# A decoder trunk on one core: the first product reads x times g, its norm is applied at the end, and set-up steps move

## The chip, the cores and the metric

The kernel runs on one core of a Trainium2 chip. The metric is the device time of one execution in microseconds (us). A core has a matrix engine (PE in the profile, with its weight loads under PEld), a vector engine (DVE), a scalar engine (ACT), a general one (POOL) and a sequencer that issues most transfers (SP). Each runs its own instructions strictly in the order in which the program wrote them, and waits on semaphores for the others.

## The reference, cut to what matters

```python
def rmsnorm(x, g):                       # x: (1, 256, 1024)
    y = x * lax.rsqrt(jnp.mean(x * x, axis=-1, keepdims=True) + EPS)
    return y * g

for l in range(2):
    h = rmsnorm(x, norm_mix_g[l])
    proj = h @ w_in[l]                   # (1024 x 6664): conv q/k, v, gates, attention q, k, v ...
    x = x + mixer(proj) @ w_out[l]       # mLSTM and sliding window attention side by side
    x = x + sqrelu_mlp(rmsnorm(x, norm_mlp_g[l]), w_up[l], w_down[l])
return rmsnorm(x, final_norm_g)
```

The columns of `w_in` that give the values `mv` are multiplied first. Row t of a product h @ w is r[t] * ((x * g) @ w)[t], where r is the reciprocal root of the row's mean square, so that r can be applied to the product instead of to x.

## The kernel before, in words

256 tokens stand in two tiles of 128 rows (`tt` 0 and 1), the 1024 features in eight blocks of 128 (`kt`). Weights come in pieces of 128 rows by 1024 columns (512 KB). A piece passes through three steps: SP loads it into a raw buffer (four of these, `N_RAW`); ACT rounds it to fp32r, the high part (`hi`, line 152); DVE subtracts that from the raw piece, the low part (`lo`, line 127, or by halves in line 134). When the low part is done the raw buffer is free, and the transfer of the piece four places on is issued (`pump_dma`). There are seven pairs of high and low buffers (`N_SPL`). Activations are split in the same way (`xh`, `xl`). A product is three matmuls: high by high, high by low, low by high. In `xs` (lines 220 to 222) the activations are stationary and 512 columns stream; in `ws` (lines 234 to 236) the weights are stationary and 256 tokens stream.

The work is a list of slots written out by hand; one slot is what one piece serves. `run_slots` (line 191) writes them out one after the other for all engines: first what was put `at` a slot, then casts of pieces up to `target` (four pieces beyond what the slot needs, or `limits`), then `late` steps, then subtractions, then `at_last`, then the slot's matmuls, then what was put `after` it. The order in this list is the order in each engine's queue.

The start, which the change touches:

- `setup_start` (line 400) issues on SP: x of tile 0 in two halves, the row of g, the first pieces, x of tile 1, and then in `small_loads` (line 388) eleven small loads. PE runs 26 and 16 small matmuls without use to warm up.
- `first_norm` (line 524) squares tile 0, takes the reciprocal root on POOL (line 349), scales x by it (line 532), transposes on PE (line 537) and splits into `xh` (ACT, line 541, with g as the scale) and `xl` (DVE, line 547). Tile 1 follows while the first slots run.
- The first product, `mv`, has slots 0 to 7. In the first half its order is by token tile (`head="t"`): slots 0 and 1 take pieces 0 to 3 for tile 0, slots 2 and 3 the same for tile 1. Slots 4 to 7 take one piece each. Its four banks are read out by `mv_evac` after slot 7: ACT takes two (line 603), DVE two (line 601).
- Slots 8 to 11 are the product `kv` (four pieces, `kk` and `kv` banks, which are the same banks that `mv_evac` empties). Slots 12 to 19 are `aq`.
- `setup_small` (line 426, at slot 2) and `setup_cols` (line 439, at slot 4) prepare masks, columns of the convolution and a table of biases, which POOL writes out and SP reads back from slot 12 on (line 462).

Of the kernel before, what the change touches and what calls it, by code (L numbers as in the profile page):

```python
# [17 lines left out]
P = 128  # L18
T = 256
# [23 lines left out]
def trunk(ctx: ExitStack, tc: tile.TileContext, x, norm_mix_g, w_in, conv_w, conv_b, b_igate, b_fgate,  # L43
# [41 lines left out]
    n_dma, n_split = [0], [0]  # L85

    def piece(w, kt, c0):
        def load(raw):
            nc.sync.dma_start(raw[:, :1024], w[kt * P : (kt + 1) * P, c0 : c0 + 1024])
# [33 lines left out]
    def pump_lo():  # L123
        for j in los:
            raw, n = raws.pop(j), pieces[j][1]
            hi, lo = pc[j]
            nc.vector.tensor_tensor(lo[:, :n], raw[:, :n], hi[:, :n].bitcast(F32), op=ALU.subtract)  # L127
# [198 lines left out]
    def hc(hf):  # L326
        return slice(hf * 512, (hf + 1) * 512)
# [55 lines left out]
    vm = const.tile([P, 2, 4, 257], F32, name="vm")  # L383
    S0 = {}

    N_WARM = (26, 16, 8)

    def small_loads():
        S0["b8"] = big8()
        rows = S0["rows"] = S0["b8"][:80, 0, 0:P]  # L390
        rb = S0["rb"] = const.tile([NB_BUCKETS, 16], F32, name="rb")
        nc.sync.dma_start(rb, rel_bias)
        for l in range(DEPTH):
            nc.sync.dma_start(gb_bias[:, l, 0:4], b_igate[l].partition_broadcast(P))
            nc.sync.dma_start(gb_bias[:, l, 4:8], b_fgate[l].partition_broadcast(P))
            nc.sync.dma_start(sink[:, l, :], attn_sinks[l].partition_broadcast(P))
            nc.sync.dma_start(rows[40 * l : 40 * l + 32, :], conv_w[l].rearrange("j (m c) -> (j m) c", c=P))
            nc.sync.dma_start(rows[40 * l + 32 : 40 * l + 40, :], conv_b[l].rearrange("(m c) -> m c", c=P))

    def setup_start():  # L400
        grow = big8()[:8, 0, 0:P]
        nc.sync.dma_start(X[:, 0, 0:512], xv[:, 0, 0:512])
        nc.sync.dma_start(X[:, 0, 512:], xv[:, 0, 512:])
        nc.sync.dma_start(grow, norm_mix_g[0].rearrange("(k c) -> k c", c=P))
        for i in range(N_RAW):
            if i == 3:
                nc.sync.dma_start(X[:, 1, :], xv[:, 1, :])
            pump_dma()
# [6 lines left out]
        nc.vector.memset(mask, 0.0)  # L415
        pw = psA()
        for _ in range(N_WARM[0]):
            nc.tensor.matmul(pw[:, :P], mask, mask, start=True, stop=True)
        pg = psA()
        nc.tensor.transpose(pg[:, :8], grow, ident[:8, :8])  # L420
        S0["gcol"] = const.tile([P, KT], F32, name="gcol")
        S0["pg"], S0["pw"] = pg, pw
        for _ in range(N_WARM[1]):
            nc.tensor.matmul(pw[:, :P], mask, mask, start=True, stop=True)

    def setup_small():
        nc.vector.tensor_copy(identb, ident)
        nc.gpsimd.affine_select(
            out=mask, in_=mask, pattern=[[1, P]], compare_op=ALU.is_ge, fill=NEG, base=0, channel_multiplier=-1)
        nc.gpsimd.memset(vm[:, :, :, 256:257], 1.0)  # L430
        z = tmp()
        nc.gpsimd.memset(z, 0.0)
        nc.scalar.copy(Rs, z[:, 0:384])
        for r in (0, 32):
            nc.gpsimd.affine_select(out=z[r : r + 32, 0:4], in_=z[r : r + 32, 0:4], pattern=[[-1, 4]],
                                    compare_op=ALU.not_equal, fill=1.0, base=0, channel_multiplier=1)
        nc.scalar.copy(sel, z[:, 0:4])

    def setup_cols():
        pt = psB()  # L440
        nc.tensor.transpose(pt[:, :80], S0["rows"], ident[:80, :80])
        nc.vector.tensor_copy(cw, pt[:, :80])
# [3 lines left out]
        nc.vector.tensor_copy(rbT, pt[:16, :NB_BUCKETS])
        Et = S0["b8"][:16, 1, 0:384]
        nc.gpsimd.memset(Et, NEG)
        bk = t5_bucket(np.arange(P))
        nc.gpsimd.tensor_copy(Et[:, 127 : 127 + 16], rbT[:, 0:16])  # L450
        for b in range(16, NB_BUCKETS):
            idx = np.nonzero(bk == b)[0]
            if len(idx):
                lo, n = int(idx[0]), len(idx)
                nc.gpsimd.tensor_copy(Et[:, 127 + lo : 127 + lo + n], rbT[:, b : b + 1].to_broadcast([16, n]))
        ed = dram.tile([16, 384], F32, name="ed")
        nc.gpsimd.dma_start(ed, Et)
        S0["ed"], S0["tz"] = ed, [big8((P, 8, T)) for _ in range(2)]
# [64 lines left out]

    def first_norm(st, xtag, nxt):

        xh, xl = st["hT"] = xT_tiles(xtag)
        N = [Norm(0), Norm(1)]
        gcol, xn, pts = S0["gcol"], {}, {}

        def scale(tt, hf):  # L530
            xn[tt, hf] = tmp()
            nc.vector.tensor_scalar(xn[tt, hf], X[:, tt, hc(hf)], N[tt].r[:, :1], None, op0=ALU.mult)

        def tr(tt, hf):
            pts[tt, hf] = psB()
            for j in range(4):
                nc.tensor.transpose(pts[tt, hf][:, j * P : (j + 1) * P], xn[tt, hf][:, j * P : (j + 1) * P], ident)

        def hi(tt, ks):
            for k in ks:  # L540
                nc.scalar.activation(xh[:, k, tt * P : (tt + 1) * P], pts[tt, k // 4][:, k % 4 * P : (k % 4 + 1) * P],  # L541
                                     AF.Copy, scale=gcol[:, k : k + 1])

        def lo(tt, ks):
            for k in ks:
                s = slice(tt * P, (tt + 1) * P)
                nc.vector.scalar_tensor_tensor(xl[:, k, s], pts[tt, k // 4][:, k % 4 * P : (k % 4 + 1) * P],
                                               gcol[:, k : k + 1], xh[:, k, s].bitcast(F32), op0=ALU.mult,
                                               op1=ALU.subtract)

        N[0].square(0)
        N[0].square(1, "dve")
        N[0].rstd()
        nc.scalar.copy(gcol, S0["pg"][:, :8])
        pump_hi(0, 0)
        scale(0, 0)
        tr(0, 0)
        for _ in range(N_WARM[2]):
            nc.tensor.matmul(S0["pw"][:, :P], mask, mask, start=True, stop=True)
# [8 lines left out]
        lo(0, (2, 3))
        pump_hi(0, 2)
        N[1].square(0)  # L570
        N[1].square(1)
        pump_lo()
        N[1].rstd()
        scale(0, 1)
        pump_hi(0, 3)
        scale(1, 0)
        pump_lo()
        scale(1, 1)

        def tr_all(tt, hf):  # L580
            tr(tt, hf)
            hi(tt, range(4 * hf, 4 * hf + 4))
            lo(tt, range(4 * hf, 4 * hf + 4))

        for i in range(4):
            limits[nxt + i] = 3 + max(0, i - 1)
        slots[nxt + 1][0].insert(2, call(lambda: tr_all(1, 0)))
        slots[nxt + 2][0].insert(1, call(lambda: tr_all(0, 1)))
        slots[nxt + 2][0].insert(4, call(lambda: tr_all(1, 1)))


    def mixer(l, ta, tb):
        w = w_in[l]
        st = {}
        s_mv = xs_group(st, "mv", "hT", w, MV0, head="t")

        def mv_evac(tt, hf):
            o = vm[:, tt, 2 * hf : 2 * hf + 2, 0:256]
            i = st[("mv", tt, hf)].rearrange("p (h c) -> p h c", h=2)
            if hf:  # L600
                nc.vector.tensor_copy(o, i)
            else:
                nc.scalar.copy(o, i)
# [462 lines left out]
    for l in range(DEPTH):  # L1066
# [95 lines left out]
```

## Time and profile before

| what | value |
|---|---|
| median of three runs | 883.37 us (883.11 to 884.58) |
| the profiled execution's own time | 884.32 us |
| its span on the core | 882.5 us |
| DVE busy, ACT busy | 572.4 us, 468.2 us |
| POOL busy | 128.3 us |
| read from memory | 153.23 MB |

The profile is of one execution. A row of a timeline gives the start, the duration, the engine, the line, what is written from what, how many in a row, and in brackets how long the engine was idle before and who ended that. A view of waits sums such idle times. A view by windows gives each engine's busy time in stretches that the reader names, with the clock that TensorE was granted (PEclk) and the share of the transfer engines. The 1.8 us between span and own time lie outside the program.

### The profile page before, as it was taken

What the parts mean: (1) busy time and instruction counts of PE and PEld (TensorE: products, weight loads), DVE (VectorE), ACT (ScalarE), POOL (GpSimd) and SP (SyncE); (2) the same over time, 40 slices, a digit from 0 to 9 for tenths busy, and PEclk for the clock granted to TensorE, in tenths of its full rate; (3) what the DMA queues carried; (4) which work ended last, traced back from release to release, by engine and by line L of the source; (5) the groups of instructions that cost most, each with busy time, mean ns of one, the idle gap of its engine ahead of it and who ended that gap; (6) DMA issues with size and microseconds to landing.
All of it is one profiled execution on the core that took longest, in us unless ns stands there. A gap on an engine that the chain in (4) does not pass through costs nothing.

```text
span 882.5 us, 15073 instructions
## 1 busy us (share of the span) xinstructions
PE 868.5 (98%) x5929; PEld 789.6 (89%) x5929; DVE 572.4 (65%) x928; ACT 468.2 (53%) x771; POOL 128.3 (15%) x164
## 2 busy tenths in 40 slices
PE   7999999999999999999999999999999999999996
PEld 5899889999989999998889997999998899999985
DVE  5758879666666654546574788876667764737363
ACT  5657776654355554544355557764634453636352
POOL 1360534120000000000002435322000000000000
PEclk9999999999999999999999999999999999999999
DMA  6875435445556747474655455354564466555621
GB/s 217 288 246 186 144 120 167 141 147 158 177 191 202 248 133 240 133 242 136 219 171 189 149 186 163 109 160 144 148 223 157 146 225 225 194 188 188 194 96 48
DMA packets 50711, 155.28 MB, mean 176 GB/s; under 512 B 7912, under 2 KB 10192, under 8 KB 50640
## 3 DMA queue, kind: packets, MB, share of 16 engines
q1 hardware_dynamic: 49456, 150.69, 52.8%
q0 software_dynamic: 896, 3.17, 1.0%
q8 instruction: 46, 0.75, 0.4%
q10 hardware_dynamic: 288, 0.46, 0.1%
q14 instruction: 25, 0.20, 0.1%
HBM read 153.23 MB, written 1.07 MB: 175 GB/s over the span
## 4 chain that ended last, share of the span: by engine, by line
PE 92%; DVE 3%; issue 2%; ACT 1%; POOL 1%; DMA 0%; POOLq 0%; SPq 0%; DVEq 0%; ACTq 0%
PE pa L220 13%; PE pa L221 13%; PE pa L222 12%; PE pa L235 10%; PE pa L234 10%; PE pa L236 10%; PE pb L235 5%; PE pb L234 5%; PE pb L236 5%; PE pb L859 1%; PE pb L322 1%; PE pb L879 1%; DVE lo L127 1%; PE pb L919 1%; PE pb L832 1%
## 5 line engine op out<-in xcount | busy, mean ns | idle before, releaser
L127 DVE TENSOR_TENSOR lo<-raw,hi 128x1024 fp32r<-128x1024 f32 (+1 forms) x276 | 332.0, 1226 | 137.5 <-ACT hi L152 134.4
L152 ACT CAST hi<-raw 128x1024 fp32r<-128x1024 f32 (+1 forms) x280 | 286.1, 1049 | 184.0 <-PE pa L222 48.1
L234 PE MATMUL pa<-xh,hi 128*128 128x256 f32 x864 | 246.4, 285 | 0.0
L235 PE MATMUL pa<-xl,hi 128*128 128x256 f32 x864 | 242.6, 281 | 0.0
L236 PE MATMUL pa<-xh,lo 128*128 128x256 f32 x864 | 241.7, 280 | 0.0
L234 PEld LDWEIGHTS pa<-xh,hi 128*128 128x128 f32 x864 | 162.7, 188 | 0.9 <-issue 0.3
L235 PEld LDWEIGHTS pa<-xl,hi 128*128 128x128 f32 x864 | 162.9, 189 | 0.3
L236 PEld LDWEIGHTS pa<-xh,lo 128*128 128x128 f32 x864 | 162.8, 188 | 0.0
L220 PE MATMUL pa<-hi,xh 128*128 128x512 f32 (+1 forms) x384 | 149.9, 390 | 1.8 <-ACT xh L541 1.8
L221 PE MATMUL pa<-lo,xh 128*128 128x512 f32 (+1 forms) x384 | 148.1, 386 | 0.5 <-DVE lo L127 0.4
L222 PE MATMUL pa<-hi,xl 128*128 128x512 f32 (+1 forms) x384 | 147.8, 385 | 0.0
L234 PE MATMUL pb<-xh,hi 128*128 128x256 f32 x384 | 107.6, 280 | 0.0
L235 PE MATMUL pb<-xl,hi 128*128 128x256 f32 x384 | 107.6, 280 | 0.0
L236 PE MATMUL pb<-xh,lo 128*128 128x256 f32 x384 | 107.3, 280 | 0.0
L220 PEld LDWEIGHTS pa<-hi,xh 128*128 128x128 f32 x384 | 72.2, 188 | 15.4 <-ACT xh L541 2.0
L222 PEld LDWEIGHTS pa<-hi,xl 128*128 128x128 f32 x384 | 72.1, 188 | 15.4
L221 PEld LDWEIGHTS pa<-lo,xh 128*128 128x128 f32 x384 | 72.2, 188 | 15.2 <-DVE lo L127 1.6
L349 POOL TENSOR_TENSOR sm<-sm,mhalf 128x1 f32<-128x1 f32 x9 | 6.6, 731 | 500.0 <-DVE sm L348 500.0
L235 PEld LDWEIGHTS pb<-xl,hi 128*128 128x128 f32 x384 | 72.3, 188 | 1.8
L234 PEld LDWEIGHTS pb<-xh,hi 128*128 128x128 f32 x384 | 72.2, 188 | 1.7
L236 PEld LDWEIGHTS pb<-xh,lo 128*128 128x128 f32 x384 | 72.3, 188 | 0.0
L220 PE MATMUL pa<-hi,b 128*128 128x512 f32 x124 | 48.8, 394 | 0.0
(210 smaller groups left out, 986.1 us busy)
## 6 DMA issues: line engine op xcount, KB each, us to landing
raw<-in_w_in SPq DMA_DIRECT2D x104, 512.0 KB, 4.5
raw<-in_w_up SPq DMA_DIRECT2D x64, 512.0 KB, 4.7
raw<-in_w_down SPq DMA_DIRECT2D x64, 512.0 KB, 4.3
raw<-in_w_branch_a SPq DMA_DIRECT2D x16, 512.0 KB, 3.5
raw<-in_w_branch_m SPq DMA_DIRECT2D x16, 512.0 KB, 4.1
raw<-in_w_out SPq DMA_DIRECT2D x16, 512.0 KB, 4.5
b<-ed SPq DMA_DIRECT2D x4, 512.0 KB, 5.2
g<-in_mlstm_norm_g POOLq DMA_DIRECT2D x2, 512.0 KB, 5.8
```

The costliest lines, as they stand in the source:

```text
L127: nc.vector.tensor_tensor(lo[:, :n], raw[:, :n], hi[:, :n].bitcast(F32), op=ALU.subtract)
L152: nc.scalar.copy(hi[:, :n], raw[:, :n])
L220: nc.tensor.matmul(b, xh[:, kt, s], wh[:, c], start=first, stop=False)
L221: nc.tensor.matmul(b, xh[:, kt, s], wl[:, c], start=False, stop=False)
L222: nc.tensor.matmul(b, xl[:, kt, s], wh[:, c], start=False, stop=last)
L234: nc.tensor.matmul(o, wh[:, c], xh[:, kt, :], start=first and half == 0, stop=False, skip_group_check=True)
L235: nc.tensor.matmul(o, wh[:, c], xl[:, kt, :], start=False, stop=False, skip_group_check=True)
L236: nc.tensor.matmul(o, wl[:, c], xh[:, kt, :], start=False, stop=last, skip_group_check=True)
L322: nc.tensor.transpose(pt[:, j * P : (j + 1) * P], src[:, j * P : (j + 1) * P], ident)
L832: nc.tensor.matmul(sp[:, P : 3 * P], q[:, P:T], kh[:, gk, :], start=False, stop=False, skip_group_check=True)
L859: nc.tensor.transpose(tp[:, j * P : (j + 1) * P], L[:, j * P : (j + 1) * P], ident)
L879: nc.tensor.matmul(o, va[:, 0, vs], PT[:, 0:T], start=(h0 % 4 == 0), stop=False, skip_group_check=True)
```

## The change

It rearranges the start of the first layer only.

- **The product without the norm.** `first_norm` transposes x itself, multiplies by g on DVE (`times_g`, 128x512 from PSUM into `xg`), and splits that into `uh`, `ul`. The product `mv` reads these (`hU`), and `mv_evac` multiplies by r while it empties the banks. For all later products the normed activations are made at slots 6 and 7: `rows` spreads r over a tile with two matmuls and an ACT copy, `normed(c)` multiplies half of `xg` by it (128x1024 on DVE) and splits the result (128x1024 on ACT and on DVE).
- **Order of the first product.** `head="k"`: each of slots 0 to 3 takes one piece for both token tiles.
- **Pieces.** Piece 0 is loaded and split in two halves. `limits` lets slots 0 to 4 split up to piece 1, 2, 3, 4 and 5 (before: 3, 3, 4, 5 in slots 0 to 3, none in slot 4).
- **Norms.** The squares of both tiles move behind the splitting of slots 2 and 3.
- **Loads.** The first halves of both x tiles come first, then pieces 0 to 2, then the second halves of x, then piece 3; the row of g is issued by ACT; six small loads instead of eleven, without spreading over partitions (a matmul with ones in `setup_cols` does that, and two more DVE copies).
- **Set-up.** `setup_small` goes from slot 2 to slot 8, its ACT copies to slot 10, `setup_cols` from slot 4 to slot 5. Warm-up matmuls: 22, 6 and 14 instead of 26, 16 and 8.

```diff
-        def load(raw):
-            nc.sync.dma_start(raw[:, :1024], w[kt * P : (kt + 1) * P, c0 : c0 + 1024])
+        def load(raw, parts=1):
+            for a in range(0, 1024, 1024 // parts):
+                b = a + 1024 // parts
+                nc.sync.dma_start(raw[:, a:b], w[kt * P : (kt + 1) * P, c0 + a : c0 + b])
...
+        gates = row[:, 0:16].rearrange("p (l c) -> p l c", l=DEPTH)
+        nc.sync.dma_start(gates[:, :, 0:4], b_igate.unsqueeze(0))
+        nc.sync.dma_start(gates[:, :, 4:8], b_fgate.unsqueeze(0))
+        nc.sync.dma_start(row[:, 16:48], attn_sinks.rearrange("(o l) h -> o (l h)", o=1))
...
     def setup_start():
         grow = big8()[:8, 0, 0:P]
+        nc.scalar.dma_start(grow, norm_mix_g[0].rearrange("(k c) -> k c", c=P))
+        for tt in range(2):
+            nc.sync.dma_start(X[:, tt, 0:512], xv[:, tt, 0:512])
+        pump_dma(2)
+        pump_dma()
+        pump_dma()
+        for tt in range(2):
+            nc.sync.dma_start(X[:, tt, 512:], xv[:, tt, 512:])
+        pump_dma()
         small_loads()
...
     def setup_cols():
         pt = psB()
         nc.tensor.transpose(pt[:, :80], S0["rows"], ident[:80, :80])
         nc.vector.tensor_copy(cw, pt[:, :80])
+        ptr = psB()
+        nc.tensor.transpose(ptr[:16, :NB_BUCKETS], S0["rb"], ident[:NB_BUCKETS, :NB_BUCKETS])
         pt = psB()
+        nc.tensor.matmul(pt[:, :48], ones[0:1, 0:1].to_broadcast([1, P]), S0["row"], start=True, stop=True)
+        nc.vector.tensor_copy(gb_bias, pt[:, 0:16].rearrange("p (l c) -> p l c", l=DEPTH))
+        nc.vector.tensor_copy(sink, pt[:, 16:48].rearrange("p (l h) -> p l h", l=DEPTH))
...
+        def times_g(tt, hf):
+            nc.vector.tensor_tensor(xg[sl(tt, hf)], pts[tt, hf].rearrange("p (k t) -> p k t", k=4),
+                                    gcol[:, 4 * hf : 4 * hf + 4].unsqueeze(2).to_broadcast([P, 4, P]), op=ALU.mult)
+        def hi(tt, hf):
+            nc.scalar.copy(uh[sl(tt, hf)], xg[sl(tt, hf)])
+        def lo(tt, hf):
+            nc.vector.tensor_tensor(ul[sl(tt, hf)], xg[sl(tt, hf)], uh[sl(tt, hf)].bitcast(F32), op=ALU.subtract)
...
+        times_g(0, 0)
+        hi(0, 0)
+        times_g(1, 0)
+        pump_hi_part(0, 512)
+        lo(0, 0)
+        hi(1, 0)
         pump_lo_part(0, 512)
+        lo(1, 0)
+        pump_hi_part(512, 1024)
         pump_lo_part(512, 1024)
         pump_lo_done()
         pump_hi(0, 1)
         pump_lo()
...
+        u = slots[nxt][0]
+        u[1], u[2] = u[2], u[1]
+        limits[nxt] = 1
+        for i in range(1, 5):
+            limits[nxt + i] = 1 + i
+        for tt in range(2):
+            slots[nxt + 1 + tt][0].insert(2, call(lambda tt=tt: rest(tt)))
+            at_last(nxt + 2 + tt, lambda tt=tt: norm(tt))
...
+        def rows():
+            pr = psB()
+            for tt in range(2):
+                nc.tensor.matmul(pr[:, tt * P : (tt + 1) * P], N[tt].r[:, 0:1].to_broadcast([P, P]), ident, start=True,
+                                 stop=True, skip_group_check=True)
+            S0["R"] = tmp()
+            nc.scalar.copy(S0["R"][:, 0:T], pr[:, 0:T])
+            st["hT"] = xT_tiles(xtag)
+        def normed(c):
+            s = (slice(None), slice(4 * c, 4 * c + 4), slice(None))
+            nc.vector.tensor_tensor(xg[s], xg[s], S0["R"][:, 0:T].unsqueeze(1).to_broadcast([P, 4, T]), op=ALU.mult)
+            evac_split(xg[s], st["hT"][0][s], st["hT"][1][s])
+        at(nxt + 6, rows)
+        at(nxt + 6, lambda: normed(0))
+        at(nxt + 7, lambda: normed(1))
...
-        s_mv = xs_group(st, "mv", "hT", w, MV0, head="t")
+        s_mv = xs_group(st, "mv", "hT" if l else "hU", w, MV0, head="t" if l else "k")
...
+            if l == 0:
+                r = S0["r"][tt]()
+                if hf:
+                    nc.vector.tensor_scalar(o, i, r, None, op0=ALU.mult)
+                else:
+                    nc.scalar.activation(o, i, AF.Copy, scale=r)
...
-            at(s_mv + 2, setup_small)
-            at(s_mv + 4, setup_cols)
+            at(s_mv + 8, setup_small)
+            at(s_mv + 10, setup_copies)
+            at(s_mv + 5, setup_cols)
```

`rest(tt)` transposes, multiplies and splits the second half of a tile, `norm(tt)` is its two squares (ACT) and `rstd`.

More of the change, by code (lines that the diff above doesn't have):

```diff
@@ L117, in pump_dma @@
             raws[j] = wp.tile([P, 1040], F32, tag="raw", bufs=N_RAW, name=nm("raw"))
-            pieces[j][0](raws[j])
+            pieces[j][0](raws[j], *parts)
             n_dma[0] += 1
@@ L129, in pump_lo, with pump_hi_part @@
         los.clear()
+    def pump_hi_part(a, b):
+        j = n_split[0] - (1 if a else 0)
+        if not a:
+            pc[j] = tuple(wp.tile([P, 1040], F32R, tag=t, bufs=N_SPL, name=nm(t)) for t in ("hi", "lo"))
+            los.append(j)
+            n_split[0] += 1
+        nc.scalar.copy(pc[j][0][:, a:b], raws[j][:, a:b])
     def pump_lo_part(a, b):
@@ L415, in setup_start @@
         nc.vector.memset(mask, 0.0)
-        pw = psA()
+        pw = S0["pw"] = psA()
         for _ in range(N_WARM[0]):
             nc.tensor.matmul(pw[:, :P], mask, mask, start=True, stop=True)
[L419 to L424, printed above, removed]
+        S0["grow"] = grow
     def setup_small():
@@ L524, in first_norm @@
     def first_norm(st, xtag, nxt):
-        xh, xl = st["hT"] = xT_tiles(xtag)
+        uh, ul = st["hU"] = xT_tiles("xb")
+        xg = big8((P, KT, T))
         N = [Norm(0), Norm(1)]
[L528 to L532, printed above, removed]
+        gcol = const.tile([P, KT], F32, name="gcol")
+        pts = {}
         def tr(tt, hf):
@@ L536, in tr @@
             for j in range(4):
[L537 to L559, printed above, removed]
+                c = hf * 512 + j * P
+                nc.tensor.transpose(pts[tt, hf][:, j * P : (j + 1) * P], X[:, tt, c : c + P], ident)
+        def sl(tt, hf):
+            return (slice(None), slice(4 * hf, 4 * hf + 4), slice(tt * P, (tt + 1) * P))
@@ L560, in first_norm @@
+        nc.vector.tensor_copy(gcol, pg[:, :8])
+        for tt in range(2):
+            tr(tt, 0)
+            for _ in range(N_WARM[1 + tt]):
+                nc.tensor.matmul(S0["pw"][:, :P], mask, mask, start=True, stop=True)
+        times_g(0, 0)
[4 more added lines that the diff above has]
+        hi(1, 0)
         pump_lo_part(0, 512)
-        hi(0, (0, 1))
-        lo(0, (0, 1))
+        lo(1, 0)
+        pump_hi_part(512, 1024)
         pump_lo_part(512, 1024)
@@ L565, in first_norm, with rest, norm @@
         pump_hi(0, 1)
-        hi(0, (2, 3))
         pump_lo()
[L568 to L589, printed above, removed]
+        def rest(tt):
+            tr(tt, 1)
+            times_g(tt, 1)
+            hi(tt, 1)
+            lo(tt, 1)
+        def norm(tt):
+            N[tt].square(0)
+            N[tt].square(1)
+            N[tt].rstd()
+        u = slots[nxt][0]
[6 more added lines that the diff above has]
+            at_last(nxt + 2 + tt, lambda tt=tt: norm(tt))
+        S0["r"] = [lambda tt=tt: N[tt].r[:, :1] for tt in range(2)]
+        def rows():
+            pr = psB()
+            for tt in range(2):
+                nc.tensor.matmul(pr[:, tt * P : (tt + 1) * P], N[tt].r[:, 0:1].to_broadcast([P, P]), ident, start=True,
[10 more added lines that the diff above has]
+        at(nxt + 7, lambda: normed(1))
     def mixer(l, ta, tb):
```

40 lines of the change are left out of this document (18 added, 22 removed).

## The prediction

> **What bounds the kernel now.** I read the page first, for what the whole is made of.
>
> ```profile
> span 882.5 us, 15073 instructions
> ...
> PE 868.5 (98%) x5929; PEld 789.6 (89%) x5929; DVE 572.4 (65%) x928; ACT 468.2 (53%) x771; POOL 128.3 (15%) x164
> ...
> PE 92%; DVE 3%; issue 2%; ACT 1%; POOL 1%; DMA 0%; POOLq 0%; SPq 0%; DVEq 0%; ACTq 0%
> ```
>
> PE is busy in 98% of the span and carries 92% of the chain that ended last. So the time is PE's stream plus its holes, and an edit at the start pays by as much as it brings forward, or sets back, the moment from which PE runs on without a hole. The timeline of PE shows the holes.
>
> ```profile
> 9.21 0.50 PE L220 MATMUL pa<-hi,xh 128*128 128x512 f32 x1 [1.79 <-ACT xh L541]
> ...
> 11.93 0.50 PE L221 MATMUL pa<-lo,xh 128*128 128x512 f32 x1 [0.16 <-DVE lo L127]
> ...
> 15.56 0.66 PE L537 MATMUL pb<-ident,tmp 128*128 128x128 f32 x4 [0.56 <-DVE tmp L532]
> ...
> 16.68 0.50 PE L221 MATMUL pa<-lo,xh 128*128 128x512 f32 x1 [0.23 <-DVE lo L127]
> ...
> 24.39 0.23 PE L441 MATMUL pb<-ident,b 80*128 80x80 f32 x1
> ...
> 24.68 0.51 PE L220 MATMUL pa<-hi,xh 128*128 128x512 f32 x1
> ...
> 35.87 0.28 PE L234 MATMUL pa<-xh,hi 128*128 128x256 f32 x1
> ...
> 37.12 0.39 PE L220 MATMUL pa<-hi,xh 128*128 128x264 f32 x1
> ...
> 87.18 0.44 PE L859 MATMUL pb<-ident,L 128*128 128x128 f32 x2 [0.57 <-POOL L L853]
> ```
>
> The first product begins at 9.21, after 1.79 us of waiting; inside it PE waits for low parts (11.93, 16.68) and for the scaled x of tile 1 (15.56). From 24.68 to 35.87 there are 48 matmuls, four slots of 12, without a hole: 2.80 us a slot. At 35.87 begins `kv`; its second token tile (264 columns) at 37.12. The next hole is at 87.18. From 37.12 on, then, whatever the start gains or loses at that matmul goes into the end, less at most the 0.57 of the later hole, which I take as unchanged since its chain begins with `kv` too.
>
> Why 9.21? The timelines of ACT and DVE:
>
> ```profile
> 3.44 0.63 ACT L342 ACTIVATE tmp<-X 128x512 f32<-128x512 f32 x1 [1.22 <-DMA X<-in_x]
> ...
> 7.85 1.04 ACT L152 CAST hi<-raw 128x1024 fp32r<-128x1024 f32 x1 [3.01 <-DMA raw<-in_w_in]
> ...
> 29.85 1.06 ACT L152 CAST hi<-raw 128x1040 fp32r<-128x1040 f32 x1 [1.59 <-DMA raw<-in_w_in]
> ...
> 35.10 1.07 ACT L603 COPY vm<-pa 128x512 f32<-128x512 f32 x2
> ...
> 36.05 2.00 ACT L152 CAST hi<-raw 128x1024 fp32r<-128x1024 f32 x2
> ```
>
> ```profile
> 4.09 0.69 DVE L344 CUSTOM_DVE_ANT_0 tmp<-X 128x512 f32<-128x512 f32 x1 [3.10 <-DMA X<-in_x]
> ...
> 5.78 0.49 DVE L532 TENSOR_SCALAR tmp<-X,sm 128x512 f32<-128x512 f32 x1 [0.67 <-POOL sm L349]
> ...
> 8.93 0.69 DVE L134 TENSOR_TENSOR lo<-raw,hi 128x512 fp32r<-128x512 f32 x1 [2.66 <-ACT hi L152]
> ...
> 25.78 0.24 DVE L442 COPY cw<-pb 128x80 f32<-128x80 f32 x1
> ...
> 25.93 0.17 DVE L446 COPY rbT<-pb 16x32 f32<-16x32 f32 x1
> ...
> 26.02 3.51 DVE L127 TENSOR_TENSOR lo<-raw,hi 128x1024 fp32r<-128x1024 f32 x3
> ...
> 36.39 1.28 DVE L601 COPY vm<-pa 128x512 f32<-128x512 f32 x2
> ```
>
> Halves of x land at 3.44 and 4.09, piece 0 at 7.85. It is the piece and its cast (1.04), not the norm, that opens the first product; a half piece costs DVE 0.69. Casts in a row take 1.00 each, subtractions 1.17. At the end of the first product ACT empties banks from 35.10 and DVE from 36.39. The first DVE copy, half of 1.28, ends at about 37.05, and the matmul at 37.12 follows it: here DVE's queue already stands level with PE. This is the place that decides.
>
> **The change, part by part.**
>
> *The front.* The square, root and scale leave the path to the first matmul; piece 0's first half takes their place. x halves now land at 3.44 and 4.09 (same places in SP's queue); four transposes take 0.66 (15.56), the multiplication by g about what the half subtraction takes (0.69), the cast of 512 columns about the 0.63 of the square at 3.44, so `uh` stands at about 5.5. The first half of piece 0 is third in the queue. At the earliest it lands one spacing of two such halves (0.65) after 4.09, at 4.75; at the latest one such spacing before 7.85, at 7.2. I take 5.4, nearer the first, since the row of g no longer lies between x and the piece in this queue. With a half cast of 0.6 the first matmul starts at 6.1, 3.1 us earlier than now. Low parts then hold slot 0 for about 0.8; it ends at 9.7.
>
> *Slots 1 to 4.* Each now needs one new piece instead of two.
>
> ```profile
> 9.13 0.33 SPq L397 DMA_DIRECT2D b<-in_conv_w  x1
> ...
> 14.81 2.17 SPq L89 DMA_DIRECT2D raw<-in_w_in  x4
> ...
> 25.89 0.37 SPq L108 DMA_DIRECT2D raw<-in_w_in  x1
> ...
> 45.19 0.43 SPq L462 DMA_DIRECT2D b<-ed  x1
> ```
>
> ```profile
> SPq L397 <- DMA raw<-in_w_in: 0.9, 1, 0.9
> ```
>
> SP has eight transfers under way: the thirteenth issue (9.13) waited for the fifth, which is piece 1, so that lands at 9.1 now. In the change no more bytes go before it; the bounds are 9.1 and 6.7 (4.75 + 0.65 + a whole piece at twice 0.65), I take 8.0, the middle. Cast 1.05 and subtraction 1.22 give the low part at 10.35, and slot 1's second matmul at 10.4: a hole of 0.45. From there 11 matmuls (2.57), three slots (8.4) and two sets of transposes:
>
> ```profile
> 18.82 0.44 PE pb L537 x4
> ```
>
> two at 0.44. Slot 5 starts at 10.4 + 2.57 + 8.4 + 0.86 = 22.2, where it starts at 24.68 + 2.80 = 27.5 now. The rest of tile 0 and 1 (0.69 + 0.63 + 0.69 each) and the four squares (0.63 each and a short read) fill ACT and DVE there, but pieces 2 to 5 are split before PE wants them, and the roots on POOL, which is idle then, are done before slot 5, `rows` wants them after it. The closest is piece 4, at 19.5 for a slot that starts at 19.4. Its transfer goes out behind six small loads instead of eleven (14.81 now), by about 11, and lands by 15: covered by the norm's steps, and PE would wait 1 us per us that it is later than about 17.
>
> *Set-up that moves.* POOL:
>
> ```profile
> 14.70 0.52 POOL L432 MEMSET tmp<- 128x512 f32 x1
> ...
> 28.37 4.13 POOL L455 COPY b<-rbT 16x3 f32<-16x3 f32 x16
> ...
> 32.80 0.71 POOL L457 DMA_DIRECT2D ed<-b  x1 [0.30 <-POOL b L455]
> ```
>
> The table takes POOL 6.6 us after `rbT`, which comes at about 23.2 instead of 26.1, so it is written by 30.5; SP reads it at 45.19. `setup_small` (0.52 and smaller fills) queues behind it and is done by 33, before ACT's copies at slot 10, which ACT reaches at about 38. Nobody waits: nothing. Without that cover ACT would stand, and slots 12 on behind it. The two new copies in `setup_cols` cost DVE as `rbT` does, 0.17 each, the matmul with ones PE about the 0.23 of row 24.39. The row of g on ACT's queue delays its table load by one issue (0.33 to 0.43 in SP's rows), 1 us before ACT has work.
>
> *Slots 5 to 7, where it is given back.* PE needs 0.47 + 3 x 2.80 for them and about 0.5 for the two matmuls of `rows` (no row; 0.2 as the transposes at 24.39, 1.0 at most by two 512-column ones): it would reach `kv` at 31.6, 4.3 before now. But DVE's queue has between the first copy of `setup_cols`, which waits for PE at 22.2, and `mv_evac`: three small copies, low parts of pieces 6 to 9, the product with r (128x1024, no row; as a subtraction, 1.22, of the same shape), the low part of the normed half, piece 10, the second product with r, its low part, piece 11. Six subtractions lie there now, ten instructions of that size then, and each `normed` makes DVE wait for one cast of ACT, since its next instruction needs it. In times: copies until 23.1; low parts of 6, 7, 8 until 26.5; piece 9's transfer goes out after low part 5 (21.7) and takes 3.96, as 25.89 to 29.85 in the rows, so cast 25.7 to 26.7 and low part until 28.0; product 29.1; cast on ACT 30.2; low part 31.5; piece 10 until 32.6; second product 33.7; cast on ACT 34.8; then ACT casts piece 11 until 35.7 and only now empties its first bank, until 36.2. `kv`, which writes that bank, starts at 36.3: PE stands for 4.7 us, behind ACT, which stood behind DVE. DVE: second low part until 36.05, piece 11 until 37.15, first bank until 37.75. `kv`'s second tile starts at 37.8 where it starts at 37.12 now.
>
> How long a transfer takes at its shortest and longest, by a median of the page and by a cast that waited for one issued at 14.81:
>
> ```profile
> raw<-in_w_branch_a SPq DMA_DIRECT2D x16, 512.0 KB, 3.5
> ```
>
> ```profile
> 20.35 1.05 ACT L152 CAST hi<-raw 128x1024 fp32r<-128x1024 f32 x1 [1.85 <-DMA raw<-in_w_in]
> ```
>
> *Sum.* +0.7 us on the profiled execution's 884.32, so 885.0; that execution lay 0.95 above the median of 883.37, which becomes 884.1. Bounds: piece 1 landing at 6.7 or 9.1 moves it by -0.45 or +1.1; piece 9's transfer at 3.5 or 5.5 (these two rows) by -0.4 or +1.6; the product with r at 0.98 (twice the 0.49 of the scaling at 5.78) by -0.5; `rows` hides behind DVE. Together -0.7 to +2.2, that is 882.7 to 885.6.
>
> *What the hole does to the clock.*
>
> ```profile
> 874.00:876.00 2.00, 0.20 (x2) 0.00 (x0) 1.42 (x5) 0.51 (x2) 0.00 (x0) 1.00 0.06 23
> ...
> 878.00:879.00 1.00, 0.00 (x0) 0.00 (x0) 0.65 (x2) 0.45 (x1) 0.00 (x0) 0.86 0.00 0
> 879.00:880.00 1.00, 0.00 (x0) 0.00 (x0) 0.00 (x0) 0.00 (x0) 0.00 (x0) 0.50 0.68 253
> ```
>
> PE's last matmul ends at 874.2 (0.20 busy in that stretch); the granted clock stays 1.00, is 0.86 on average in the stretch from 878 and then 0.50: it falls by half some 4.5 us after the last matmul, and it did not fall in the hole of 1.79. My hole of 4.7 lies past that, if just. The Trainium skill, "TensorE: Matmul & The Clock Gate" (Part 1), has a rule against such a hole: the clock is halved after one idle window of about 3.4 us, the windows run freely, and it comes back after a busy one. By it a hole of 4.7 us would hold a whole window in about 4 of 10 executions, an estimate from that page; the fall after 4.5 us agrees with it. The rows alone bound it: no fall at 1.79, one at 4.5. What it costs is seen at the kernel's first matmuls:
>
> ```profile
> 1.04 2.95 PE L418 MATMUL pa<-mask 128*128 128x128 bf16 x26 [1.04 <-DVE mask L415]
> ...
> 6.82 0.61 PE L559 MATMUL pa<-mask 128*128 128x128 bf16 x8
> ```
>
> 26 in 2.95 us (0.113 each) against eight in 0.61 (0.076): it takes about 4 us until they run at the later pace. Four us at half speed are 2.0 us lost. The sum is 884.1 without and 886.1 with it.
>
> **The rivals.**
>
> *The clock falls in the hole before `kv`* (slower): 886.1. For it: the hole is as long as the idle time after which the clock fell. Against it: only just; a hole at the short end of my bounds would be 4 us, and the one fall in the rows needed 4.5. It decides from about there, so less than even.
>
> *ACT and DVE keep up* (faster): if `normed` fits beside pieces 6 to 11, PE goes through at 31.6 and the 4.3 us stay: 879.1. For it: DVE is idle 35% of the span. Against it: the queue is in order, and bank reads stand last in it; ten instructions of 1.17, the copies and two waits for a cast make 14 us on DVE beside PE's 9.4.
>
> *Pieces come no earlier* (the front does not gain): piece 0's halves at 7.2 and 7.85, piece 1 at 9.1. The first matmul comes at 7.9, slot 5 at 23.3 and `kv` 1.1 later: 885.2. For it: transfers share the same engines and no byte is saved before piece 1. Against it: x's halves came 0.65 apart.
>
> **How the numbers follow.** A difference under about 0.2% (1.8 us) can't be told from none here. My forecast has 0.47, the clock 0.32, ACT and DVE keeping up 0.13, late pieces 0.08. Faster comes from ACT and DVE keeping up alone, 0.13. Slower: 0.27 of the clock's (a late fall leaves 0.05 inside), 0.06 of the forecast's upper end and 0.06 of the late pieces', 0.39; the rest is 0.48. The time is the forecast's, 884.1. The range goes from 882.4, the forecast's lower end with a little for a shorter queue, to 887.0, which takes in the clock's case with its own upper end of about 1 more; outside lie most of the 0.13 and some of the clock's, under 0.2. The forecast's own range is 882.7 to 885.6.
>
> **What would show it.** Right: the first xs matmul at about 6, slot 5's transposes at about 22, then a hole of 4 to 5 us at `kv`, put down to ACT's read of a bank (line of `mv_evac`), with DVE and ACT busy or waiting for each other all through it. Wrong: no hole there (the second rival), a first matmul after 7.5, or piece 4 or 9 waited for by PE. The granted clock by windows after the hole tells the first rival.

## The result, and the profile after

| | median | span of the runs | ratio to before, 95% interval |
|---|---|---|---|
| before | 884.22 us | 883.11 to 884.58 (7 runs) | |
| changed | 886.49 us | 885.72 to 886.95 (7 runs) | 1.0028 [1.0019, 1.0038] |

The changed kernel is 2.3 us slower: outside the forecast's own range, inside the whole range, and where the rival of the clock lay (886.1). The profiled execution took 885.72 us with a span of 883.9.

The timeline of PE in the changed kernel; the brackets give the idle time before and who ended it:

```profile
7.21 0.48 PE L230 MATMUL pa<-hi,xh 128*128 128x512 f32 x1
8.29 0.50 PE L231 MATMUL pa<-lo,xh 128*128 128x512 f32 x1 [0.60 <-DVE lo L144]
...
11.18 0.40 PE L231 MATMUL pa<-lo,xh 128*128 128x512 f32 x1
...
22.93 0.23 PE L454 MATMUL pb<-ident,b 80*128 80x80 f32 x1
...
32.10 0.40 PE L232 MATMUL pa<-hi,xl 128*128 128x512 f32 x1
37.21 0.39 PE L244 MATMUL pa<-xh,hi 128*128 128x256 f32 x1 [4.71 <-ACT vm L643]
...
38.41 0.42 PE L230 MATMUL pa<-hi,xh 128*128 128x264 f32 x1
...
50.38 0.28 PE L244 MATMUL pa<-xh,hi 128*128 128x256 f32 x1
...
90.08 0.44 PE L904 MATMUL pb<-ident,L 128*128 128x128 f32 x2 [0.58 <-POOL L L898]
...
875.14 0.28 PE L232 MATMUL pb<-hi,b 128*128 128x256 f32 x1
```

The first product begins at 7.21, 2.0 us earlier than before, and slot 5 (the transpose of line 454) at 22.93, 4.6 us earlier than the 27.5 before. All of that and more is lost in one hole: 4.71 us ahead of `kv`, ended by ACT's read of a bank (line 643, `mv_evac`). `kv` begins at 37.21, its second token tile at 38.41 (before: 35.87 and 37.12). The later hole is the old one, 0.58.

What stood in the two queues meanwhile, ACT first, then DVE:

```profile
26.44 1.06 ACT L162 CAST hi<-raw 128x1040 fp32r<-128x1040 f32 x1 [1.22 <-DMA raw<-in_w_in]
...
29.94 1.05 ACT L323 CAST xh<-b 128x1024 fp32r<-128x1024 f32 x1 [2.17 <-DVE b L622]
30.90 1.06 ACT L162 CAST hi<-raw 128x1040 fp32r<-128x1040 f32 x1
34.57 1.04 ACT L323 CAST xh<-b 128x1024 fp32r<-128x1024 f32 x1 [2.61 <-DVE b L622]
35.52 1.05 ACT L162 CAST hi<-raw 128x1040 fp32r<-128x1040 f32 x1
36.48 1.26 ACT L643 ACTIVATE vm<-pa,sm 128x512 f32<-128x512 f32 x2
```

```profile
27.53 1.24 DVE L129 TENSOR_TENSOR lo<-raw,hi 128x1040 fp32r<-128x1040 f32 x1 [0.19 <-ACT hi L162]
28.69 1.22 DVE L622 TENSOR_TENSOR b<-b,tmp 128x1024 f32<-128x1024 f32 x1
31.02 1.23 DVE L324 TENSOR_TENSOR xl<-b,xh 128x1024 fp32r<-128x1024 f32 x1 [1.11 <-ACT xh L323]
32.17 1.23 DVE L129 TENSOR_TENSOR lo<-raw,hi 128x1040 fp32r<-128x1040 f32 x1
33.32 1.22 DVE L622 TENSOR_TENSOR b<-b,tmp 128x1024 f32<-128x1024 f32 x1
35.65 1.23 DVE L324 TENSOR_TENSOR xl<-b,xh 128x1024 fp32r<-128x1024 f32 x1 [1.11 <-ACT xh L323]
36.79 1.33 DVE L129 TENSOR_TENSOR lo<-raw,hi 128x1040 fp32r<-128x1040 f32 x1
38.04 1.40 DVE L641 TENSOR_SCALAR vm<-pa,sm 128x512 f32<-128x512 f32 x2
```

They pass the work back and forth. ACT's cast at 29.94 waited 2.17 us for DVE's product with r (line 622); DVE then waited 1.11 us for that cast; the same again at 34.57 and 35.65. PE had done its last `mv` matmul at 32.5, yet ACT reads the first bank only at 36.48.

The page's busy shares don't show what came on top (PE is at 98% as before, all 40 digits of its clock row are 9). A view by windows does; its columns are the stretch, the busy times of PE, PEld, DVE, ACT and POOL, then the granted clock, the share of the transfer engines and GB/s:

```profile
30.72:34.13 3.41, 1.78 (x8) 1.12 (x6) 3.11 (x3) 1.24 (x2) 3.41 (x6) 1.00 0.53 209
34.13:37.54 3.41, 0.33 (x2) 0.33 (x3) 2.30 (x3) 2.97 (x4) 3.10 (x7) 1.00 0.69 219
37.54:40.95 3.41, 3.41 (x18) 3.41 (x17) 3.41 (x6) 3.41 (x6) 0.74 (x4) 0.50 0.76 239
40.95:44.36 3.41, 3.41 (x31) 3.41 (x30) 3.25 (x3) 1.17 (x2) 0.00 (x0) 1.00 0.76 237
```

From 37.54 to 40.95, just when `kv` has begun, TensorE runs at 0.50: 18 matmuls in 3.41 us, against 31 in the next stretch of the same length. So `aq`, which began at 47.70 before, begins at 50.38: 2.7 us later, half of it by the hole, half by the clock.

### The profile page after: what moved, and what is told of

The parts are those of the page before. It is cut to its first block, busy times and chain, and to the rows that moved or that the text cites. A ratio compares the mean times of both kernels' runs of the same rounds, so it can differ in the third digit from the quotient of the medians.

```text
span 883.9 us, 15055 instructions
## 1 busy us (share of the span) xinstructions
PE 868.0 (98%) x5927; PEld 791.7 (90%) x5927; DVE 575.7 (65%) x921; ACT 468.8 (53%) x764; POOL 133.1 (15%) x165
## 4 chain that ended last, share of the span: by engine, by line
PE 83%; DVE 6%; ACT 3%; issue 3%; DMA 2%; POOL 2%; SPq 0%; POOLq 0%; DVEq 0%; ACTq 0%
PE pa L231 11%; PE pa L230 11%; PE pa L232 11%; PE pa L244 9%; PE pa L245 9%; PE pa L246 9%; PE pb L245 5%; PE pb L244 5%; PE pb L246 5%; DVE lo L129 2%; PE pb L904 1%; ACT hi L162 1%; PE pb L924 1%; PE pb L332 1%; DMA raw<-in_w_in 1%
## 5 line engine op out<-in xcount | busy, mean ns | idle before, releaser
L230 PEld LDWEIGHTS pa<-hi,xh 128*128 128x128 f32 x384 | 72.5, 189 | 13.2 <-issue 0.3
L231 PE MATMUL pa<-lo,b 128*128 128x512 f32 x124 | 48.9, 395 | 0.0
```

What stands on the lines that cost most here:

```text
L230: nc.tensor.matmul(b, xh[:, kt, s], wh[:, c], start=first, stop=False)
L231: nc.tensor.matmul(b, xh[:, kt, s], wl[:, c], start=False, stop=False)
```

## The experiments

Theory at the outset: the hole comes from the order in the queues (the bank reads stand behind work for later products), and the clock's fall in it costs another 2 us. Rivals: the early part sets the time (pieces, the start of slot 5), or the fall costs nothing that counts. The ratios are to runs of the kernel before beside them (medians 883.79 to 883.93).

**1. The second half of the norm one slot later.**

```diff
-        at(nxt + 7, lambda: normed(1))
+        at(nxt + 8, lambda: normed(1))
```

> normed(1) goes from slot 7 to slot 8, behind the bank reads of the first product. Theory (the bank reads stand behind normed(1) in the queues of DVE and ACT, and the hole that this makes lets the clock fall): ACT reads the first bank after piece 11's cast, at about 33.0 instead of 36.5, kv starts at about 33.7 instead of 37.2, the hole shrinks from 4.7 to about 1.2, the clock stays at 1.00 from about 7 to the end of the matmuls, and the time falls by 3.5 and by 1.5 to 3 for the clock: about 881 us, under the kernel before. Rival (the loss comes from the front: later pieces, other loads): kv gains nothing lasting, 886.5.

Measured: 881.11 us (880.91 to 881.86), 0.9969 [0.9958, 0.9981]. PE in this kernel:

```profile
34.41 0.39 PE L244 MATMUL pa<-xh,hi 128*128 128x256 f32 x1 [0.73 <-ACT vm L643]
...
36.13 0.39 PE L230 MATMUL pa<-hi,xh 128*128 128x264 f32 x1 [0.38 <-DVE vm L641]
```

The bank reads now stand ahead of the second product, and 4.71 us of hole become 0.73 and 0.38; the granted clock stays at 1.00. One step in the list of slots makes the same work 5.4 us faster than the changed kernel. The order is the cause of the hole.

**2. Idle matmuls in the hole**, and nothing else changed.

```diff
+        def keep_warm():
+            pk = psB()
+            for _ in range(64):
+                nc.tensor.matmul(pk[:, :P], mask, mask, start=True, stop=True)
+        after(nxt + 7, keep_warm)
```

> 64 matmuls of 128 columns without use stand between slot 7 and slot 8, in a bank of their own; nothing else moves. Theory: kv still starts at about 37.2, since DVE and ACT set it, but the clock doesn't fall, and kv's 96 matmuls take 11.6 us as before the change: 886.5 less 1.5 to 3, about 884. Rival (the hole alone is the loss, the clock costs nothing): 886.5 or slightly more.

Measured: 884.34 us (883.44 to 884.67), 1.0005 [0.9996, 1.0013].

```profile
31.44 3.75 PE L632 MATMUL pb<-mask 128*128 128x128 bf16 x64
36.16 0.38 PE L244 MATMUL pa<-xh,hi 128*128 128x256 f32 x1 [0.98 <-ACT vm L650]
...
48.35 0.28 PE L244 MATMUL pa<-xh,hi 128*128 128x256 f32 x1
```

`kv` still waits for ACT, but the clock holds: from 36.16 to `aq` it takes 12.2 us (48.35 - 36.16), where the changed kernel takes 13.2 (50.38 - 37.21) with one window at 0.50, and 14.2 in its second trace (number 10) with two. The difference of the two medians is 2.1 us (886.49 - 884.34): that is the price of the fall, known to about 1 us by the two intervals, and what is left without it can't be told from no change. None of the 14 executions of the changed kernel (885.36 to 886.95, with those of number 10) lies near 884.34, so the fall came in all of them, as far as their times tell. That `kv` comes 1.1 us earlier in this trace is no effect of the edit: piece 9 came 1.1 us earlier too (its cast at 25.37), as it does from one execution to the next. From that cast to `kv` it is 10.8 us in both.

**3. Without the products with r.**

```diff
-            nc.vector.tensor_tensor(xg[s], xg[s], S0["R"][:, 0:T].unsqueeze(1).to_broadcast([P, 4, T]), op=ALU.mult)
```

> Leaves out the two multiplications by r (128x1024 on DVE) in normed, so that later products read x times g without the norm; the rest of the queue stays. Theory: two instructions of 1.15 leave DVE ahead of the bank reads, kv starts at about 34.9, the hole is 2.4 and too short for the clock: 886.5 - 2.3 - 2 = about 882. Rival (transfers of pieces 8 to 11 set the pace and DVE has slack): kv within 0.5 of 37.2, about 886.

This kernel leaves the norm out of all later products, so it serves for its time alone.

Measured: 880.38 us (879.59 to 881.02), 0.9960 [0.9947, 0.9972]; `kv` at 32.39.

```profile
26.70 1.05 ACT L323 CAST xh<-b 128x1024 fp32r<-128x1024 f32 x1
28.05 1.06 ACT L162 CAST hi<-raw 128x1040 fp32r<-128x1040 f32 x1 [0.30 <-DMA raw<-in_w_in]
```

I had counted the two products at little more than their own length, 2.4 us. `kv` comes 4.8 us earlier (37.21 - 32.39), of which 1.0 is again an earlier piece 9 (25.47); 3.8 are left, and the medians agree (886.49 - 880.38 = 6.1, less 2.1 for the clock). Without the products ACT's cast (26.70) doesn't wait for DVE at all, where it waited 2.17 and 2.61 us, and DVE doesn't stand for ACT's casts, 1.11 us twice. That and the 2.4 would be 4.6; the last two pieces now wait for their transfers instead (0.30 at 28.05). A step of a chain that goes from DVE to ACT and back costs its own time and the time that DVE stands for the answer.

**4. The set-up of the columns one slot earlier**, for the rival that slot 5's copies open the chain.

```diff
-            at(s_mv + 5, setup_cols)
+            at(s_mv + 4, setup_cols)
```

> setup_cols back at slot 4, the rest as changed. Theory in its simple form (DVE's count from slot 5 on): the copies are gone before piece 5's low part, DVE starts piece 6 at 22.4 instead of 23.85 and kv comes 1.4 earlier: about 884. The finer form: piece 9 lands at 26.4 whatever DVE did before, its low part stays at 27.5, and nothing behind it moves: 886.5. Rival of both (set-up costs by itself): kv moves with the 0.7 us of copies, 885.8.

Measured: 886.17 us (885.56 to 887.09), 1.0026 [1.0017, 1.0035]. Nothing gained: DVE does the copies some 3 us earlier and pieces 6 to 8 between 1.2 and 1.9 us earlier, and then waits for piece 9. ACT in this kernel:

```profile
26.72 1.06 ACT L162 CAST hi<-raw 128x1040 fp32r<-128x1040 f32 x1 [1.88 <-DMA raw<-in_w_in]
```

Piece 9 comes at 26.72, as in the changed kernel (26.44), and the chain starts from it. The windows of this one are of use below:

```profile
31.40:34.81 3.41, 0.75 (x4) 0.26 (x2) 3.41 (x3) 0.93 (x1) 0.00 (x0) 1.00 0.56 208
34.81:38.22 3.41, 0.63 (x3) 0.63 (x4) 2.30 (x3) 3.27 (x5) 0.00 (x0) 0.50 0.45 148
38.22:41.64 3.42, 3.42 (x17) 3.42 (x17) 3.42 (x6) 3.23 (x5) 0.00 (x0) 0.50 0.51 156
```

**5. A piece's subtraction between the product and its low part**, so that DVE has work while ACT casts.

```diff
-        at(nxt + 6, lambda: normed(0))
-        at(nxt + 7, lambda: normed(1))
+        at(nxt + 6, lambda: scaled(0))
+        at_last(nxt + 6, lambda: split(0))
+        at(nxt + 7, lambda: scaled(1))
+        at_last(nxt + 7, lambda: split(1))
```

`scaled` is the product with r, `split` the cast and the low part.

> Both normed steps stay at slots 6 and 7, but the split of each half stands behind the cast and the low part of piece 10 and 11 instead of ahead of them, so that DVE has a piece to do while ACT casts the normed half. Theory (each wait of DVE for that cast, 1.1 us twice, is part of the hole): bank reads come 2.1 earlier, kv at about 35.2, a hole of 2.6, too short for the clock in most executions: 886.5 - 2.1 - 2 = about 882.3. Rival (only the number of instructions ahead of the bank reads counts, not the waits): nothing moves, 886.2.

Measured: 883.55 us (882.17 to 884.79), 0.9995 [0.9986, 1.0004], a miss by 1.2 us. The queues did as expected: the hole is 2.58 us and `kv` begins at 35.02. But the windows show a fall that I hadn't expected in so short a hole:

```profile
31.90:35.31 3.41, 0.82 (x5) 0.39 (x4) 3.41 (x4) 2.58 (x4) 3.41 (x4) 1.00 0.68 250
35.31:38.73 3.42, 3.42 (x18) 3.42 (x18) 3.42 (x6) 2.11 (x3) 3.10 (x13) 0.50 0.56 161
```

**6. The same with 36 idle matmuls in the hole** (`keep_warm` again), to see whether that fall is the miss.

```diff
+            for _ in range(36):
+                nc.tensor.matmul(pk[:, :P], mask, mask, start=True, stop=True)
```

> The kernel with the casts between (a hole of 2.59 us before kv, 883.55, the clock fell all the same) with 36 idle matmuls in that hole (about 2.1 us by 64 of them in 3.75). Theory that its missing gain was the clock's fall: no window at half clock, kv where it was (35.0), the time 1 to 1.5 lower, 882.2 (881.8 to 882.6). Theory that the hole was too short for the clock to matter, and the missing gain lies elsewhere: 883.5 as before.

Measured: 882.12 us (881.78 to 884.67), 0.9984 [0.9975, 0.9993], as the clock's theory has it.

```profile
32.37 2.18 PE L635 MATMUL pb<-mask 128*128 128x128 bf16 x36
35.28 0.39 PE L244 MATMUL pa<-xh,hi 128*128 128x256 f32 x1 [0.73 <-ACT vm L657]
```

`kv` starts no earlier (35.28), the clock stays at 1.00 through it, and the missing 1.4 us are there (883.55 - 882.12). The two intervals overlap, but the executions of experiment 5 say the same among themselves: eight had a mean granted clock of 0.993 to 0.995 and took 883.28 to 884.79 us, and the one with 0.998, which leaves hardly any room for the fall, took 882.26 (two at 0.996 took 882.17 and 883.69). Work without use, put into a hole, pays.

**7 and 8. Both orders together, and piece 11 behind the bank reads.** Number 7 is experiment 5 with the second half at slot 8; number 8 also holds back one more piece, with the last line:

```diff
-        at(nxt + 7, lambda: scaled(1))
-        at_last(nxt + 7, lambda: split(1))
+        at(nxt + 8, lambda: scaled(1))
+        at_last(nxt + 8, lambda: split(1))
+        limits[nxt + 7] = 10
```

> The same order inside the slot, and the second half at slot 8 behind the bank reads. Theory: kv at 33.0 to 33.5 and no wait left at its second tile, where e1 had 34.4 and 36.1: 1 to 2 under e1's 881.1, about 879.6. Rival: PE's own end of slot 7 (32 to 33.7, by when the pieces land at the start) is the bound now, no gain over 881.1.

> As the one before, and piece 11 is split in slot 8 instead of slot 7, so that its cast and low part stand behind the bank reads too. Theory: bank reads come another 1 earlier on both engines, as far as PE's own end of slot 7 lets them: 0 to 0.7 under the one before, about 879.3. Rival (the second normed half and piece 11 now come late for kv's third and fourth slot): a wait of PE there and a time over the one before.

Measured: 879.98 us (879.82 to 880.24), 0.9955 [0.9943, 0.9968], and 879.23 us (878.96 to 879.49), 0.9947 [0.9933, 0.9960]. ACT in number 8:

```profile
30.16 0.69 ACT L652 ACTIVATE vm<-pa,sm 128x512 f32<-128x512 f32 x1
31.23 0.69 ACT L652 ACTIVATE vm<-pa,sm 128x512 f32<-128x512 f32 x1 [0.38 <-PE pa L232]
```

Now ACT waits for PE (31.23), not PE for ACT. PE runs into `kv` at 31.67 without a hole, the 31.6 of my second rival. This version beats both kernels.

**9. The first product by token tile**, with pieces split as far ahead as that asks: the opposite rival, that the early part sets the time.

```diff
-            limits[nxt + i] = 1 + i
+            limits[nxt + i] = min(2 + i, 5)
...
-        s_mv = xs_group(st, "mv", "hT" if l else "hU", w, MV0, head="t" if l else "k")
+        s_mv = xs_group(st, "mv", "hT" if l else "hU", w, MV0, head="t")
```

> The changed kernel with the order by token tile in the first four slots as before the change (head t; limits 3, 4, 5, 5 in slots 1 to 4, since slot 1 now needs pieces 2 and 3). Theory (slot 5's start sets when DVE takes up the pieces, and so kv): piece 3, which lands at 12.2, holds slot 1 until about 15, slot 5 starts about 2 later than 22.9, kv about 2 later than 37.2: about 888.5. Rival (DVE's chain doesn't hang on PE at slot 5): kv stays at 37.2 and the hole shrinks instead, 886 or, where the clock stays, 884.

Measured: 888.01 us (887.69 to 891.18), 1.0055 [1.0042, 1.0069].

```profile
26.12 0.23 PE L454 MATMUL pb<-ident,b 80*128 80x80 f32 x1
...
40.13 0.58 PE L244 MATMUL pa<-xh,hi 128*128 128x256 f32 x1 [4.44 <-ACT vm L643]
```

Slot 5 comes 3.2 us later than in the changed kernel and `kv` 2.9 later, with much the same hole. So the early part does count, through slot 5: here DVE's first copy of the set-up waits 2.78 us for PE until 26.39, and pieces 6 to 11 stand behind it. But not all of the 3.2 us is the order. In this execution the clock fell early as well, while PE waited for pieces, and again in the hole:

```profile
6.92:10.34 3.42, 2.04 (x13) 0.98 (x10) 3.27 (x6) 2.72 (x4) 0.00 (x0) 1.00 1.01 389
10.34:13.75 3.41, 2.88 (x7) 2.30 (x8) 1.86 (x3) 1.56 (x2) 0.00 (x0) 0.50 0.67 211
...
34.23:37.64 3.41, 1.46 (x7) 0.84 (x5) 3.22 (x3) 0.79 (x2) 3.41 (x5) 1.00 0.61 226
```

Between 10.88 and 13.60 matmuls start up to 0.43 us apart, where 0.23 is usual, which makes some 1.3 of the 3.2 us. Taking one piece a slot is worth some 1.5 us by the medians (888.01 - 886.49), early falls of the clock included; the five executions, 887.69 to 891.18, are spread more widely than those of any other kernel here.

**10. Each kernel once more**, since in all traces of the changed family the stretch from `aq` to the end was shorter than in the trace of before.

> The kernel before, unchanged, for a second trace of it. Question: in all traces so far that stem from the changed kernel the stretch from the first matmul of aq to the last matmul of the kernel takes 824.8 to 825.5 us; in the one trace of before it took 826.5. Theory that single executions differ so: this trace gives a length between, and the time lies at 883.9 again. Theory that the changed kernel also gains some 1.5 us behind aq (from what its set-up leaves queued or placed in memory): 826.0 to 826.8 again.

> The changed kernel, unchanged, for a second trace and a ratio on the same chip as the next one. Theory of the clock's fall: 886 to 887, a hole of 4.2 to 5 us before kv, the granted clock 0.5 for one or two windows of 3.41 us within 3.4 us of kv's start. If the fall came only in some executions, some of the times would lie near 884.3, where the kernel with idle matmuls in the hole lay.

Measured: before 883.85 us (883.39 to 884.45), 1.0002 [0.9993, 1.0011]; changed 886.38 us (885.36 to 886.68), 1.0028 [1.0017, 1.0038]. In the second trace of the changed kernel the hole is 5.12 us, two windows are at 0.50 (36.22 to 43.05), and `kv` to `aq` takes from 37.30 to 51.50. The first matmul of `aq` and the last of the kernel, in the second trace of before:

```profile
46.71 0.28 PE L234 MATMUL pa<-xh,hi 128*128 128x256 f32 x1
...
873.22 0.28 PE L222 MATMUL pb<-hi,b 128*128 128x256 f32 x1
```

That is 826.5 us between the two starts (the expectations count to the end of the last one, 0.28 more); in the changed kernel's rows above it is 875.14 - 50.38 = 824.8, in its second trace 824.5. The changed kernel does gain some 1.7 us, in a stretch that the change doesn't touch. No hole makes it: from one matmul to the next the starts differ there by at most 0.3 us, at one place (ahead of line 904), and that place differs as much between two traces of one kernel.

**11. The kernel before with the memory layout of the changed one.** The changed kernel keeps one more constant (`z2`), which moves every buffer behind it by 32 bytes, and takes the pair of activation buffers `xb` first, which gives both pairs, and buffers laid out behind them, other places.

```diff
+        const.tile([P, 4], F32, name="z2")
...
-        xh, xl = st["hT"] = xT_tiles(xtag)
+        xT_tiles("xb")
...
         N[0].square(0)
+        xh, xl = st["hT"] = xT_tiles(xtag)
```

> The kernel before with the memory layout of the changed one and nothing else of it: 16 bytes per partition that no instruction uses (32 with their alignment), which push the raw, high and low buffers 32 bytes up, and the split activations at the places that they have in the changed kernel. No instruction is added or moved. Question: both traces of before take 826.5 and 826.8 us from aq's first matmul to the last one, all traces that stem from the changed kernel 824.8 to 825.5; the difference lies in single matmuls, 0.012 us each, the same ones in every execution. Theory of the places (which buffer a matmul reads at which address sets its pace): that stretch falls to 824.8 to 825.1 and the time by about 1.7, to 882.2 (881.6 to 882.7). Rival, the order of the set-up or of the banks: 826.5 to 826.8 and 883.8 (883.4 to 884.4).

Measured: 882.48 us (881.62 to 883.11), 0.9983 [0.9974, 0.9992].

```profile
47.24 0.28 PE L234 MATMUL pa<-xh,hi 128*128 128x256 f32 x1
...
168.90 0.28 PE L235 MATMUL pa<-xl,hi 128*128 128x256 f32 x1
...
169.96 0.28 PE L235 MATMUL pa<-xl,hi 128*128 128x256 f32 x1
...
872.14 0.28 PE L222 MATMUL pb<-hi,b 128*128 128x256 f32 x1
```

The stretch is 824.9 us. The same matmuls in the first trace of before:

```profile
47.70 0.28 PE L234 MATMUL pa<-xh,hi 128*128 128x256 f32 x1
...
168.92 0.29 PE L235 MATMUL pa<-xl,hi 128*128 128x256 f32 x1
...
170.02 0.29 PE L235 MATMUL pa<-xl,hi 128*128 128x256 f32 x1
...
873.92 0.28 PE L222 MATMUL pb<-hi,b 128*128 128x256 f32 x1
```

Here it is 826.2. Nine matmuls, three of them by the low part of x, took 1.10 us (168.92 to 170.02) and take 1.06 with the buffers moved (168.90 to 169.96): some 0.01 us each for the three, too little for any view to name, over some 5,700 matmuls of which a part is concerned. Set side by side start by start over the whole stretch, the two traces of before agree within 2 ns at all but 17 places, and before and this kernel differ by more at some 970. So the layout is worth 1.4 us of the total. Which of the two moves does it, and by what rule of addresses, stays open.

## Why the prediction was right and wrong

**Right: where it happens and why.** One hole, at `kv`, put down to `mv_evac` on ACT behind DVE: forecast 4.7 us, measured 4.71. The chain stood as forecast, link by link and each 0.7 to 1.0 us later: piece 9's cast at 26.44 (forecast 25.7), the first cast of the normed half until 31.0 (30.2), the second until 35.6 (34.8), ACT's first bank at 36.48 (35.7), `kv` at 37.21 (36.3). Experiment 1 shows that it is the order, experiment 3 that it is the product and its hand-overs, experiment 4 that piece 9 sets its beginning. Nobody waits for the set-up that moves to slots 8 and 10, as forecast, though POOL was later than I had it (the table written at 35.6, forecast 30.5): ACT's copy of line 449 at 39.52 has no wait, and PE has no hole from `kv` to 90.08. The later hole stayed as it was.

**Wrong: which case is likeliest.** I gave the clock's rival 0.32, because the rows of before showed a fall 4.5 us after the last matmul, and I took that length as the point from which it decides. It isn't a length. Experiments 4 and 5 and the changed kernel show falls at the end of a window of 3.41 us in which PE was busy for 0.75, 0.82 and 0.33 us; experiment 5 has a hole of 2.58. Both traces of the changed kernel have the fall. The price was right, 2.0 forecast and 2.1 by experiment 2, but partly by luck: I had taken 4 us at half speed from the first matmuls, and in the two traces `kv` ran at half for 3.4 us (37.54 to 40.95) and 5.7 (37.30 to 43.05). The Trainium skill, "TensorE: Matmul & The Clock Gate" (Part 1), says that the clock is halved after an idle window of about 3.4 us on a free-running grid. The grid agrees with these traces, the idle window doesn't: falls came after windows with matmuls in up to 1.46 us of 3.41, and once 2.04. My estimate of 4 in 10 from that rule was too low for this reason. With a limit near 1.5 us of matmuls (last section) a hole of 4.71 us, however the grid cuts it, leaves at least 2.35 us idle in one window and so 1.06 us for matmuls: by this estimate it falls every time.

**Wrong: two terms of the sum, which hid each other.** The likeliest case without the clock was +0.7 on before, and experiment 2 without the clock is +0.5. That looks like a hit and is none. Experiment 11 shows -1.4 in it that no step of the prediction has: the layout. The start alone is then about +1.9 (0.5 + 1.4), with about 1 us of noise; it is what is left over, not measured alone. The traces agree (`kv` at 37.21 and 37.30 in the two of the changed kernel, at 35.87, 34.74 and 35.27 in the three with the old start: on average 2.0 later, or 1.6 with the 36.16 of experiment 2). It lies near my upper bound of 2.2, but that bound was itself short of its own terms: 0.7 + 1.1 + 1.6 is 3.4. The mis-sized term is the front: the first matmul at 7.21 where I had 6.1, slot 1's second matmul at 11.18 where I had 10.4, slot 5 at 22.93 where I had 22.2; `kv` inherits it through low part 5 and the transfer of piece 9 behind it. The rows show where it came from: the transposes ahead of the first product took 1.11 and 1.06 us for four, where I had 0.66, so that `uh` stood at 6.20 instead of 5.5, and ACT's half cast of piece 0 stood behind it until 6.72; the 14 warm-up matmuls then held PE until 7.2. The sentence that the start's gain or loss goes into the end, less at most 0.57 for the later hole, was false: another 1.4 came from matmuls that the change doesn't mention.

The account of the whole, then: start +1.9, clock +2.1, layout -1.4, against 2.3 and 2.6 measured (884.22 to 886.49, 883.79 to 886.38). Since the start is what is left over, only the traces' 1.6 to 2.0 check this sum.

**The other rivals.** That ACT and DVE keep up (879.1) was wrong for this order and right for another: experiment 8, 879.23, though 1.4 of its 4.7 us are the layout's. That pieces come no earlier was wrong: slot 1 had piece 1 without a hole.

## What to carry to other kernels

In engines that work strictly in order, write the reads that free a bank ahead of the work for later products, and never put a chain that passes between two engines in front of them: a step that hands over twice costs its length and the wait for the answer. When a change opens a hole on TensorE, add to it the fall of the clock if the hole, or several short ones, can take up more than half of one window of 3.4 us; some matmuls without use in it are worth their instructions. When a change adds a buffer or takes buffers in another order, give the old kernel the new layout before putting a microsecond down to the idea.

## What the runs showed of the hardware

- The granted clock changes only on a grid of 3.41 us, whose place differs from execution to execution. What counts is how long PE was busy in a window. In the 14 traces there are 3,567 windows at full clock. All but one of the 20 that were followed by a fall had PE busy for 1.46 us or less (0.33, 0.75, 0.82 and 1.46 above); those that no fall followed had 1.56 or more (1.78 from 30.72 to 34.13 above). The exception is the early window of experiment 9, 2.04; why is open. The clock came back after windows with 2.88 (10.34 to 13.75 in experiment 9) and more, and stayed at half after one with 0.63 (34.81 to 38.22 in experiment 4) and one with 2.33 (36.22 to 39.63 in the second trace of the changed kernel). So a fall in these holes lasts one window or two, by where the hole ends in the grid, and cost 1.0 and 2.0 us between `kv` and `aq` in the two traces of the changed kernel.
- The place of the operands in memory changes the pace of single matmuls by about a tenth (0.01 of 0.12 us, in the rows of experiment 11) and the time of this kernel by 0.17% (0.9983 [0.9974, 0.9992]); two traces of one kernel show the same pace (826.2 and 826.5 us for the stretch before, 824.8 and 824.5 changed).
